# Scaling the first chunks from the weight's row in PSUM, and normalising retention outputs ahead of the state's split at first chunks

## The chip, the cores and the metric

The kernel runs on one core of one Trainium2 chip. The metric is the time of one execution on the device, in microseconds (us). The core has TensorE (PE) for matrix products and transpositions, VectorE (DVE), ScalarE (ACT) and GpSimd (POOL) for work by element, and SyncE (SP), which issues DMA transfers; ACT and POOL can issue them too. Each engine takes its instructions in its own order. PE writes into PSUM, which is divided into banks; DVE and ACT read it there. PE's products are made in a rounded fp32 type (`fp32r`): an operand is split into a high part and the remainder ("hi" and "lo"), and three products (hi·hi, lo·hi, hi·lo) are summed.

## The reference

Two layers, one of retention and one of sliding-window attention, over 1024 prompt rows and 8 decode rows of width 1024. The change is in the first stage and in the retention of layer 1:

```python
def rmsnorm(x, g):
    return x * lax.rsqrt(jnp.mean(x * x, axis=-1, keepdims=True) + EPS) * g

def retention_layer(x, S0, g_norm, w_in, g_out, w_out):
    h = rmsnorm(x, g_norm)                    # x 1024x1024 (prompt), 8x1024 (decode)
    q, k, v, gate = split(h @ w_in)           # widths 1024, 1024, 2048, 2048
    # 4 heads, chunks of 128 rows, per head and chunk:
    #   o_c = (q_c k_c^T * dmask) v_c + (q_c S) * cross_decay
    #   S   = S * chunk_decay + (k_c * k_decay)^T v_c
    o = rmsnorm(o, g_out)                     # per head, over 512 columns
    return x + (o * silu(gate)) @ w_out, S
```

The attention layer (16 query heads, 2 key heads, window 128, with sinks) follows; the change leaves its computation alone.

## The kernel before

**First stage.** The prompt is taken in 8 chunks of 128 rows (numbers 0 to 7); number 8 stands for the decode rows. A chunk is loaded (`xload`, L425, a DMA on SP's queue), squared and summed by ACT (`sq`, L430), its factor rsqrt(mean + eps) is made by POOL (`pw`, L434 and the power at L119), it is scaled by DVE with factor and gain (`sc`, L439), transposed by PE into two banks (`TR`, through the helper at L104), and split from there: `hi` by ACT (L456), `lo` by DVE (L460). The gain `norm_ret` comes as one row; PE multiplies it with a row of ones (L874), so that it stands in 128 partitions of the two banks `bank_of[0, 0]` and `bank_of[0, 1]`; DVE copies it from there to `gb` (L887). The decode rows are scaled like a chunk, and transposed by eight small transpositions into `p8`; `dcols` (L494, L495) appends columns of them to the operands of the products, and `rdec` keeps them all (L907). The first products of the projections are at L543; weights come into five slots of a pool (`raw_tile`, L176), and are split into `woh` (ACT, L220) and `wol` (POOL or DVE, L225).

The products of a group of output columns (a "set") are combined on DVE and ACT (`evac`, L363 to L379; the gate's SiLU at L382), and each output goes to scratch in DRAM (`spill`: for a gate set POOL applies the gain, L392, and copies the decode columns, L401; then SP issues the DMA `gsc<-raw`, L396). The last set's outputs lie in the `raw` slots, four of the five.

**Retention.** The heads go in two pairs, (0,1) and then (2,3), over 8 chunks each: 32 steps, in the order chunk by chunk with both heads of a pair. The work of a step is divided into small functions, and one loop (L1572) issues them for several steps at once, skewed:

| engine | functions (line) |
|---|---|
| PE | `b_qk` scores and transposition of k into the `tr` tile (L778, L104); `b_mm` state `S` (L1032 to L1034), output `po` (L1036 to L1045); `b_tr` transposition of the normalised output `on` |
| ACT | `b_kh` (L785), `b_sh` (L800), `b_vh` (L810), `b_qh` (L821), `b_Sh` split of the state (L1052), `b_sq` square of the output with sum (L1070), `b_oh` (L1105) |
| DVE | `b_kl` (L790), `b_sT` masked scores (L795), `b_Sl` (L1064), `b_ts` (L1074), `b_on` normalises (L1082), `b_og` times gate (L1098) |
| POOL | `b_sl` (L805), `b_vl` (L815), `b_ql` (L827), `b_pw` (power, L119), `b_ol` (L1110) |

In pass i of the loop PE's order is `b_qk(i+1)`, `b_mm(i)`, `b_tr(i-1)`; the other engines' order is set by `others(i)` (L1112): `b_og(i-2)`, the state and the norm of step i−1, the conversions of step i+1 (`CONV`) with `b_on(i-1)` after the first three, then `b_oh` and `b_ol` of step i−2. At a head's last chunk, and at a first chunk but the first of all, the norm's three functions stand ahead of the state's two. The order of ACT, DVE, POOL and SP is written out by hand: it is the order of issue in the code.

The first chunk of a head has no state to read, and the last one writes its state `sf` to the output by a DMA on ACT's queue (L1057). The `tr` tile has two slots (pool `trp`, L937), which the scores and transposition of k of one step and the transposed output of another take in turn. Steps 0 and 1 (`early`, L751) take their operands from tiles of the gate stage (`first`); from step 2 on, and for `on` and `ss` from the start, they lie in the pool `rp`, whose order in memory `lay` sets by hand (L1018):

```python
lay("Sh1", "Sl1", "sT0", "sTh0", "sTl0", "qh0", "ql0", "kh0", "kl0", "ss0", "ss1", "sT1", "on1", "kh1", "kl1",
    "pad", "on0", "vh0", "vl0", "sTh1", "sTl1", "qh1", "Sh0", "Sl0", "vh1", "vl1", "ql1")
```

A tile of `rp` waits for whatever lay on its words before, tile by tile (`reuse_waits="tile"`): at the beginning of retention those are tiles of the gate stage.

Of the kernel before, what the change touches and what calls it, by code (L numbers as in the profile page):

```python
# [7 lines left out]
F32 = mybir.dt.float32  # L8
F32R = mybir.dt.float32r
AF = mybir.ActivationFunctionType  # L10
ALU = mybir.AluOpType
PSUM = bass.MemoryType.PSUM
# [4 lines left out]
ND = 8  # L17
# [5 lines left out]
NCH = NP // C  # L23
# [44 lines left out]
def _trunk(ctx, tc, nc, a):  # L68
    x_prompt, x_sample, state_ret = a["x_prompt"], a["x_sample"], a["state_ret"]
    cache_k, cache_v = a["cache_k"], a["cache_v"]  # L70
    norm_ret, ret_out_norm, norm_swa = a["norm_ret"], a["ret_out_norm"], a["norm_swa"]
# [3 lines left out]
    y_p, y_s, nrp, nrs = a["y_p"], a["y_s"], a["nrp"], a["nrs"]  # L75
# [27 lines left out]
    def tr(out, in_, ident, start=True, stop=True):  # L103
        nc.tensor.matmul(out, in_, ident, is_transpose=True, start=start, stop=stop)  # L104


    ident = cp.tile([128, 128], F32, name="ident")
# [18 lines left out]
    B11, B21, T3, B22, T2, T1, T4 = range(7)  # L126
# [6 lines left out]
    dcp = sa.enter_context(tc.tile_pool(name="dcp", bufs=1, reuse_waits="tile"))  # L133
# [5 lines left out]
    vdp = sa.enter_context(tc.tile_pool(name="vdp", bufs=1, space=PSUM))  # L139
# [4 lines left out]
    rdec = rdec32[:, :, 0:ND]  # L144
# [13 lines left out]
    xq_ = ExitStack()  # L158
# [254 lines left out]
    junk = xq.tile([128, D], F32, name="junk")  # L413
    X, SS, PO = {}, {}, {}

    def xload(c):
        if c in (0, 1, 2):
            X[c] = xq.tile([128, D], F32, tag="xq", bufs=4, name="xq")
        elif c == 7:
            X[c] = raw_tile()  # L420
        elif c != 3:
            X[c] = sp.tile([128, D], F32, tag="u", bufs=3, name="u")
        if c == 8:
            X[c] = X[c][0:ND, :]
        nc.sync.dma_start(out=X[c], in_=x_sample[:, 0, :] if c == 8 else x_prompt[0, c * 128:c * 128 + 128, :])  # L425

    def sq(c):
        SS[c] = sp.tile([128, 1], F32, name="ss", bufs=4)
# [8 lines left out]
    def sc(c):  # L437
        n = X[c].shape[0]
        dve.scalar_tensor_tensor(X[c], X[c], SS[c][:n], gb[:n], MUL, MUL)  # L439

    def TR(c, b):

        PO[c] = [bank(b, j).rearrange("p (k t) -> p k t", k=4) for j in range(2)]
        for j in range(2):
            for k in range(4):
                tr(PO[c][j][:, k, :], X[c][:, 512 * j + k * 128:512 * j + k * 128 + 128], ident)
# [41 lines left out]
    def dcols(t, x, src=None):  # L488

        if src is None:  # L490
            k0, r0 = DB[x]
            src = rdec[:, k0:k0 + 4, r0 + 2 * t:r0 + 2 * t + 2]
        h = XH[t][x][:, :, 256:258]
        dve.tensor_copy(h, src)  # L494
        dve.tensor_tensor(XL[t][x][:, :, 256:258], src, h.bitcast(F32), SUB)  # L495
# [122 lines left out]
    n = 0  # L618
# [253 lines left out]
    for j in range(2):  # L872
        bank_of[0, j] = bank(0, j)
        mm(bank_of[0, j], row1, grow[:, 512 * j:512 * j + 512], start=True, stop=True)  # L874
    act(warm, warm, AF.Silu)
    for c in (0, 8, 2):
        xload(c)
    for r in range(2):
        raw_load(q0, r, nc.sync)
# [3 lines left out]
        raw_load(k0, r, nc.sync)  # L883
    for c in (4, 6, 7):
        xload(c)
    for j in range(2):
        dve.tensor_copy(gb[:, 512 * j:512 * j + 512], bank_of[0, j])  # L887
    for c in (0, 2, 8):
        sq(c)
        pw(c)  # L890
    sc(0)
    TR(0, 1)
    sc(2)
    TR(2, 2)
    sc(8)
    p8 = vdp.tile([128, 8, ND], F32, tag="vd", name="pd8")
    for k in range(8):
        tr(p8[:, k, :], X[8][:, k * 128:k * 128 + 128], ident[:ND, :ND])
    for j in range(2):
        hi(0, j)  # L900
        lo(0, j)
    w_hi(q0, "A11", 0)
    for j in range(2):
        hi(2, j)
    dcols(0, B11, p8[:, 0:4, 0:2])
    dcols(0, B21, p8[:, 4:8, 0:2])
    dve.tensor_copy(rdec, p8)  # L907
    for j in range(2):
        lo(2, j)
    w_lo(q0, "A11", 0, pool)  # L910
# [23 lines left out]
    print("stage", clock[0], "decode", t0)  # L934
    sa.close()
    tq = ExitStack()
    trp = tq.enter_context(tc.tile_pool(name="trp", bufs=2, space=PSUM))  # L937

    ap = ctx.enter_context(tc.tile_pool(name="ap", bufs=1, side="right", reuse_waits="tile"))
    SA = ap.tile([128, 8, 2 * NT], F32R, name="SA")  # L940
# [51 lines left out]
        else:  # L992
            pool.tensor_tensor(l_, src, h.bitcast(F32), SUB)

    spp = sb.enter_context(tc.tile_pool(name="spp", bufs=1, space=PSUM))
    ss_ = ExitStack()
    sSp = ss_.enter_context(tc.tile_pool(name="sSp", bufs=1, space=PSUM, side="right"))
    ogt = [rp0.tile([128, 4, 128], F32, name="og", tag="og%d" % n) for n in range(2)]
    rp = sb.enter_context(tc.tile_pool(name="rp", bufs=1, reuse_waits="tile"))
    rt[:] = [rp, trp]  # L1000
# [4 lines left out]
    def lay(*names):  # L1005
        for nm in names:
            if nm[:2] in ("Sh", "Sl"):
                state(nm[:2], int(nm[2]))
                continue
            if nm == "pad":  # L1010
                rp.tile([128, 72], F32, name=nm)
                continue
            n, k = nm[:-1], int(nm[-1])
            w = dict(on=DV, ss=1, sT=128, vh=DV, vl=DV, kh=DK, kl=DK, sTh=128, sTl=128, qh=256, ql=256)[n]
            t = rp.tile([128, w], F32 if n in ("on", "ss", "sT") else F32R, name=n, tag=nm)
            R.setdefault(n, [None, None])[k] = t.rearrange("p (f t) -> p f t", f=2) if n in ("qh", "ql") else t

    lay("Sh1", "Sl1", "sT0", "sTh0", "sTl0", "qh0", "ql0", "kh0", "kl0", "ss0", "ss1", "sT1", "on1", "kh1", "kl1",  # L1018
        "pad", "on0", "vh0", "vl0", "sTh1", "sTl1", "qh1", "Sh0", "Sl0", "vh1", "vl1", "ql1")
    mk["m"] += [M23[:, 0:128], M23[:, 128:256]]  # L1020
    epsg = M01[:, 288:292]

# [24 lines left out]
    def b_Sh(h, c):  # L1047
        d = heads[h]
        if c < NCH - 1:
            d["Sb"] = [state(nm, h % 2) for nm in ("Sh", "Sl")]  # L1050
            for f in range(2):
                act(d["Sb"][0][:, f], d["S"][f], AF.Copy, scale=GAM[h] ** (128.0 * (c + 1) - SREF))  # L1052
        else:
            sf = rp.tile([128, 2, DV], F32, tag="Sh%d" % (h % 2), name="sf")
            for f in range(2):
                act(sf[:, f], d["S"][f], AF.Copy, scale=GAM[h] ** SREF)
            nc.scalar.dma_start(out=nrp[0, 0, h].rearrange("(f p) e -> p f e", p=128), in_=sf)  # L1057

    def b_Sl(h, c):
        d = heads[h]  # L1060
# [51 lines left out]
    def others(i):  # L1112
        conv = [(fn, i + 1 if i + 1 > 1 else -1) for fn in CONV]
        state = [(b_Sh, i - 1), (b_Sl, i - 1)]
        norm = [(b_sq, i - 1), (b_ts, i - 1), (b_pw, i - 1)]
        turn = 0 <= i - 1 < NS and (steps[i - 1][1] == NCH - 1 or (steps[i - 1][1] == 0 and i > 2))
        for fn, n in ([(b_og, i - 2)] + (norm + state if turn else state + norm) + conv[0:3] +
                      [(b_on, i - 1)] + conv[3:] + [(b_oh, i - 2), (b_ol, i - 2)]):
            at_step(fn, n)

    def dec_gate():
# [28 lines left out]
    pq = {}  # L1150
# [375 lines left out]
    def p_open():  # L1526
        pp = ps_.enter_context(tc.tile_pool(name="pp", bufs=1, reuse_waits="tile"))

        def t512(name):
            return pp.tile([128, 4, 128], F32, name=name)  # L1530
        pq["rb"] = [pp.tile([128, 4, 256], F32, name="rb", tag=f"rb{j}") for j in range(2)]
        pq["dT"] = pp.tile([128, 7, 4, 4], F32, name="dT")
        pp.tile([128, 144], F32, name="pad")
        pq["xr"] = pp.tile([128, 16, 64], F32, name="xr")
        for key in "xp":
            pq["r" + key] = pp.tile([128, 516], F32, name="r" + key).rearrange("p (t n) -> p t n", t=2)
        s2b = t512("s2b")
        pq["s1b"] = t512("s1b")
        pq["s2ab"] = [t512("s2a"), s2b]
        w3 = pp.tile([128, 2, 4, 128], F32R, name="w3")  # L1540
        w = [pp.tile([128, 2, 4, 128], F32R, name=f"w{j}") for j in (0, 1, 2, 4)]
        pq["w"] = [[x[:, 0], x[:, 1]] for x in w[0:3] + [w3] + w[3:]]
        pq["s1a"] = t512("s1a")
        pq["b2"] = ps_.enter_context(tc.tile_pool(name="b2p", bufs=1, space=PSUM))
        pq["nw"] = 0
        pq["yz"] = [[v.rearrange("p k f -> p (k f)").rearrange("p (k n) -> p k n", k=2) for v in vs]
                    for vs in ((pq["s2ab"][0], pq["s1a"]), (pq["s2ab"][1], pq["s1b"]))]
# [74 lines left out]


    ctx.enter_context(tc.manual_schedule(engines={ET.Activation, ET.DVE, ET.Pool, ET.SP}))
    pjp = ctx.enter_context(tc.tile_pool(name="pjp", bufs=2, space=PSUM, side="right"))
    wp = ctx.enter_context(tc.tile_pool(name="wp", bufs=1, reuse_waits="tile"))

    pieces, flight, tick = [], [], [0]
# [124 lines left out]
    t16 = c2p.tile([16, 8], F32, name="t16")  # L1753
    e16 = c2p.tile([16, 8], F32, name="e16")

    scp = tq.enter_context(tc.tile_pool(name="scp", bufs=2, space=PSUM))
    msp = tq.enter_context(tc.tile_pool(name="msp", bufs=1, space=PSUM))
    kvp = ctx.enter_context(tc.tile_pool(name="kvp", bufs=1))
    atp = ctx.enter_context(tc.tile_pool(name="atp", bufs=1))
    atq = []  # L1760
# [687 lines left out]
        now()  # L2448
    tq.close()
    xq_ = ExitStack()  # L2450
    xyp = xq_.enter_context(tc.tile_pool(name="xyp", bufs=1, space=PSUM))
    pvp = xq_.enter_context(tc.tile_pool(name="pvp", bufs=1, space=PSUM))
    job()
    fill(ps, 1.0)
    xy = xy_tile()
# [99 lines left out]
        job(0)  # L2555
    xq_.close()
    tq = ctx.enter_context(ExitStack())
    trp = tq.enter_context(tc.tile_pool(name="trp", bufs=2, space=PSUM))
    msp = tq.enter_context(tc.tile_pool(name="msp", bufs=1, space=PSUM))
    attn[0] = False  # L2560
    drain(out)

# [37 lines left out]
```

## Time and profile before

| quantity | value |
|---|---|
| three runs | 1236.3, 1239.33 and 1242.99 us, median 1239.33 |
| profiled execution: time | 1237.02 us |
| profiled execution: span in the trace | 1235.2 us |
| PE busy | 1214.5 us (98%) |
| DVE, POOL, ACT busy | 741.2, 701.2, 588.8 us |
| first product of the projections starts | 14.42 us |
| PE idle before the transpositions of `on` of step 0, and of step 16 | 1.79 and 0.78 us |

The span is the stretch from the first to the last recorded instruction; the execution's own time is 1.8 us longer. "Idle before" an instruction is the time in which its engine had nothing to do just ahead of it, with what ended that time. A tile's name is the program's: `on` the normalised output, `S` the state, `po` the output in PSUM, `kh` and `kl` the two parts of k, `sT` the masked scores, `ss` sums and factors.

### The profile page before, as it was taken

The numbers are of one execution on the slowest core, as the hardware profiler recorded it, in microseconds if no ns is written. First come the engines' busy times: TensorE is split into PE (matmuls) and PEld (weight loads), VectorE is DVE, ScalarE is ACT, GpSimd is POOL, SyncE is SP. The second block draws the span as 40 slices with busy tenths as digits, with TensorE's granted clock in tenths as the row PEclk, the third lists the DMA queues.
The fourth block names the chain that finished last, engine by engine and source line by source line (L and its number), as shares of the span: only waits on it lengthen the run. The fifth ranks groups of instructions, "written<-read, shape, count | busy, mean of one in ns | idle before, by whom it ended". The sixth has DMA issues, their size and how long they took to land.

```text
span 1235.2 us, 29414 instructions
## 1 busy us (share of the span) xinstructions
PE 1214.5 (98%) x11297; PEld 1152.4 (93%) x11297; DVE 741.2 (60%) x1425; ACT 588.8 (48%) x1511; POOL 701.2 (57%) x763
## 2 busy tenths in 40 slices
PE   8999999999999999999999999999999999999898
PEld 7999999999999999988888999999989999999898
DVE  6954656556566667357676455677336676577432
ACT  6533444544545655368876123455554546544000
POOL 6654543545638889889877145682655548545010
PEclk9999999999999999999999999999999999999999
DMA  6313867768686775455687894685531447255364
GB/s 220 113 48 120 248 186 218 227 199 231 188 254 178 196 237 171 126 175 170 214 270 209 248 253 168 194 244 148 130 97 58 133 131 184 78 172 168 76 135 86
DMA packets 260027, 213.11 MB, mean 173 GB/s; under 512 B 72881, under 2 KB 230901, under 8 KB 259870
## 3 DMA queue, kind: packets, MB, share of 16 engines
q1 hardware_dynamic: 215376, 178.75, 49.2%
q10 hardware_dynamic: 44510, 32.47, 8.7%
q8 instruction: 89, 1.46, 0.5%
q14 instruction: 52, 0.43, 0.1%
HBM read 139.03 MB, written 73.17 MB: 172 GB/s over the span
## 4 chain that ended last, share of the span: by engine, by line
PE 88%; DMA 4%; DVE 3%; POOL 2%; issue 1%; ACT 1%; SPq 1%; ACTq 0%; POOLq 0%; DVEq 0%
PE S L1317 9%; PE b L334 8%; PE b L336 7%; PE b L335 7%; PE pj L1692 7%; PE pj L1694 6%; PE pj L1693 6%; PE b L327 4%; PE b L328 4%; PE b L329 4%; PE b L543 2%; PE xy L2052 2%; PE tr L104 2%; PE o L2110 2%; PE S L334 1%; PE S L335 1%
## 5 line engine op out<-in xcount | busy, mean ns | idle before, releaser
L334 PE MATMUL b<-xh,woh 128*128 128x258 f32 x784 | 223.4, 285 | 0.0
L336 PE MATMUL b<-xh,wol 128*128 128x258 f32 x784 | 222.2, 283 | 1.0 <-POOL wol L225 1.0
L335 PE MATMUL b<-xl,woh 128*128 128x258 f32 x784 | 221.9, 283 | 0.0
L1692 PE MATMUL pj<-SA,wh 128*128 128x384 f32 (+1 forms) x576 | 190.1, 330 | 3.5 <-DVE sq L2338 2.0
L1694 PE MATMUL pj<-SA,wl 128*128 128x384 f32 (+1 forms) x576 | 185.1, 321 | 0.0
L1693 PE MATMUL pj<-SA,wh 128*128 128x384 f32 (+1 forms) x576 | 184.4, 320 | 0.0
L334 PEld LDWEIGHTS b<-xh,woh 128*128 128x128 f32 x784 | 148.2, 189 | 4.1 <-issue 4.1
L336 PEld LDWEIGHTS b<-xh,wol 128*128 128x128 f32 x784 | 148.1, 189 | 1.4 <-POOL wol L225 1.4
L335 PEld LDWEIGHTS b<-xl,woh 128*128 128x128 f32 x784 | 148.8, 190 | 0.0
L225 POOL TENSOR_TENSOR wol<-raw,woh 128x512 fp32r<-128x512 f32 x51 | 66.6, 1313 | 119.5 <-ACT woh L220 108.3
L327 PE MATMUL b<-woh,xh 128*128 128x256 f32 x448 | 126.8, 283 | 0.0
L328 PE MATMUL b<-wol,xh 128*128 128x256 f32 x448 | 126.2, 282 | 0.0
L329 PE MATMUL b<-woh,xl 128*128 128x256 f32 x448 | 125.8, 281 | 0.0
L1692 PEld LDWEIGHTS pj<-SA,wh 128*128 128x128 f32 x576 | 108.6, 189 | 11.7 <-issue 5.8
L1693 PEld LDWEIGHTS pj<-SA,wh 128*128 128x128 f32 x576 | 109.0, 189 | 0.0
L1694 PEld LDWEIGHTS pj<-SA,wl 128*128 128x128 f32 x576 | 108.8, 189 | 0.0
L327 PEld LDWEIGHTS b<-woh,xh 128*128 128x128 f32 x448 | 84.4, 188 | 5.0 <-issue 2.9
L1650 POOL TENSOR_TENSOR wl<-wr,wh 128x512 fp32r<-128x512 f32 x48 | 63.0, 1322 | 38.2 <-DMA out_dram<-yo 17.3
L329 PEld LDWEIGHTS b<-woh,xl 128*128 128x128 f32 x448 | 84.4, 188 | 0.0
L328 PEld LDWEIGHTS b<-wol,xh 128*128 128x128 f32 x448 | 84.4, 188 | 0.0
L220 ACT ACTIVATE woh<-s 128x512 fp32r<-128x512 f32 x88 | 54.1, 624 | 60.3 <-POOL s L210 24.0
L225 DVE TENSOR_TENSOR wol<-s,woh 128x512 fp32r<-128x512 f32 x88 | 67.9, 775 | 21.3 <-ACT woh L220 21.0
(515 smaller groups left out, 3156.4 us busy)
## 6 DMA issues: line engine op xcount, KB each, us to landing
raw<-in_w_in_ret_dram ACTq DMA_DIRECT2D x44, 512.0 KB
st<-in_state_ret_dram SPq DMA_DIRECT2D x64, 256.0 KB
out_dram<-st SPq DMA_DIRECT2D x64, 256.0 KB
vb<-vscr SPq DMA_DIRECT2D x64, 128.0 KB
evp<-qks SPq DMA_DIRECT2D x32, 256.0 KB
evx<-vsc SPq DMA_DIRECT2D x32, 256.0 KB
wr<-in_w_in_swa_dram SPq DMA_DIRECT2D x32, 256.0 KB
pbs<-pb SPq DMA_DIRECT2D x16, 320.0 KB
```

The lines of the kernel that those rows point to most:

```text
L225: eng.tensor_tensor(lo, src_of(s, name, sub), hi.bitcast(F32), SUB)
L327: mm(dst, xh, wh, start=a and i == 0, stop=False, skip_group_check=True)
L328: mm(dst, xh, wl, start=False, stop=False, skip_group_check=True)
L329: mm(dst, xl, wh, start=False, stop=z, skip_group_check=True)
L334: mm(dst, wh, xh, start=a, stop=False, **sg)
L335: mm(dst, wh, xl, start=False, stop=False, **sg)
L336: mm(dst, wl, xh, start=False, stop=z, **sg)
L1317: mm(box[0], s.op[f"A{i + 1}{j + 1}", 0][w][:, k, :], xs_[t][x[j]][:, k, :], start=(xs_ is XH and w == 0 and j + k == 0), stop=(xs_ is XL ...
L1650: nc.gpsimd.tensor_tensor(box["lo"][:, js, :], raw, box["hi"].bitcast(F32)[:, js, :], ALU.subtract)
L1692: mm(ps, hi[:, k, fs], xh[:, k, t0:t1], start=first and k == ks[0], stop=False)
L1693: mm(ps, hi[:, k, fs], xl[:, k, t0:t1], start=False, stop=False)
L1694: mm(ps, lo[:, k, fs], xh[:, k, t0:t1], start=False, stop=last and k == ks[-1])
```

## The change

At the start:

- x8 (the decode rows) is loaded on ACT's queue instead of SP's, and with it, on the same queue, a new small tile `g8`: the gain as 8 rows of 128. The squares and factors come in the order 8, 0, 2 instead of 0, 2, 8.
- `g8` is transposed to `gk8` (128x8). The decode rows are scaled by their factor alone, transposed, and `rdec` is made from the transposed rows times `gk8`; `dcols` takes its columns from `rdec`.
- Chunks 0 and 2 are scaled in halves directly from the gain's row in PSUM (`sc_first`). The copies of the gain to `gb` go from DVE to ACT, one after each half of chunk 2.

In retention:

- In passes 1 and 17 (after the first chunk of head 0 and of head 2) the order is norm, `b_on`, then the state, then all conversions. The `b_oh` and `b_ol` of step 14 are issued in pass 17 instead of 16.
- `on0` lies first in `rp`.
- The final states `sf` are issued on SP's queue instead of ACT's.

Besides, the PSUM pools `trp`, `spp`, `sSp`, `b2p`, `pjp`, `scp`, `msp`, `xyp` and `pvp` (and `trp` and `msp` once more at the end) get `reuse_waits="tile"`.

```diff
-    def xload(c):
+    def xload(c, eng=nc.sync):
...
-        nc.sync.dma_start(out=X[c], in_=x_sample[:, 0, :] if c == 8 else ...)
+        eng.dma_start(out=X[c], in_=x_sample[:, 0, :] if c == 8 else ...)
...
+    def sc_first(c, j):
+        v = X[c][:, 512 * j:512 * j + 512]
+        dve.scalar_tensor_tensor(v, v, SS[c], bank_of[0, j], MUL, MUL)
...
+    xload(8, nc.scalar)
+    g8 = dcp.tile([8, 128], F32, name="g8")
+    nc.scalar.dma_start(out=g8, in_=norm_ret.rearrange("o (k p) -> (o k) p", p=128))
     act(warm, warm, AF.Silu)
-    for c in (0, 8, 2):
+    for c in (0, 2):
         xload(c)
...
-    for j in range(2):
-        dve.tensor_copy(gb[:, 512 * j:512 * j + 512], bank_of[0, j])
-    for c in (0, 2, 8):
+    for c in (8, 0, 2):
         sq(c)
         pw(c)
-    sc(0)
-    TR(0, 1)
-    sc(2)
-    TR(2, 2)
-    sc(8)
-    p8 = vdp.tile([128, 8, ND], F32, tag="vd", name="pd8")
+    p8 = vdp.tile([128, 9, ND], F32, tag="vd", name="pd8")
+    tr(p8[:, 8, :], g8, ident[:8, :8])
+    gk8 = dcp.tile([128, 8], F32, name="gk8")
+    dve.tensor_copy(gk8, p8[:, 8, :])
+    dve.tensor_scalar(X[8], X[8], SS[8][:ND], None, MUL)
     for k in range(8):
         tr(p8[:, k, :], X[8][:, k * 128:k * 128 + 128], ident[:ND, :ND])
+    for j in range(2):
+        sc_first(0, j)
+    TR(0, 1)
+    dve.tensor_tensor(rdec, p8[:, 0:8, :], gk8.unsqueeze(2).broadcast_to([128, 8, ND]), MUL)
+    for j in range(2):
+        sc_first(2, j)
+        act(gb[:, 512 * j:512 * j + 512], bank_of[0, j], AF.Copy)
+    TR(2, 2)
+    dcols(0, B11)
+    dcols(0, B21)
     for j in range(2):
         hi(0, j)
         lo(0, j)
     w_hi(q0, "A11", 0)
     for j in range(2):
         hi(2, j)
-    dcols(0, B11, p8[:, 0:4, 0:2])
-    dcols(0, B21, p8[:, 4:8, 0:2])
-    dve.tensor_copy(rdec, p8)
...
-    trp = tq.enter_context(tc.tile_pool(name="trp", bufs=2, space=PSUM))
+    trp = tq.enter_context(tc.tile_pool(name="trp", bufs=2, reuse_waits="tile", space=PSUM))
...
-    lay("Sh1", "Sl1", ..., "kl1", "pad", "on0", "vh0", ...)
+    lay("on0", "Sh1", "Sl1", ..., "kl1", "pad", "vh0", ...)
...
-            nc.scalar.dma_start(out=nrp[0, 0, h].rearrange("(f p) e -> p f e", p=128), in_=sf)
+            nc.sync.dma_start(out=nrp[0, 0, h].rearrange("(f p) e -> p f e", p=128), in_=sf)
...
-        turn = 0 <= i - 1 < NS and (steps[i - 1][1] == NCH - 1 or (steps[i - 1][1] == 0 and i > 2))
-        for fn, n in ([(b_og, i - 2)] + (norm + state if turn else state + norm) + conv[0:3] +
-                      [(b_on, i - 1)] + conv[3:] + [(b_oh, i - 2), (b_ol, i - 2)]):
+        on = [(b_on, i - 1)]
+        og = [(b_oh, i - 2), (b_ol, i - 2)]
+        if i in (1, NS // 2 + 1):
+            seq = norm + on + [(b_oh, i - 3), (b_ol, i - 3)] + state + conv + og
+        else:
+            turn = 0 <= i - 1 < NS and (steps[i - 1][1] == NCH - 1 or (steps[i - 1][1] == 0 and i > 2))
+            seq = (norm + state if turn else state + norm) + conv[0:3] + on + conv[3:] + (og if i != NS // 2 else [])
+        for fn, n in [(b_og, i - 2)] + seq:
             at_step(fn, n)
```

More of the change, by code (lines that the diff above doesn't have):

```diff
@@ L424, in xload @@
             X[c] = X[c][0:ND, :]
-        nc.sync.dma_start(out=X[c], in_=x_sample[:, 0, :] if c == 8 else x_prompt[0, c * 128:c * 128 + 128, :])
+        eng.dma_start(out=X[c], in_=x_sample[:, 0, :] if c == 8 else x_prompt[0, c * 128:c * 128 + 128, :])
     def sq(c):
@@ L993, in dec_cols @@
             pool.tensor_tensor(l_, src, h.bitcast(F32), SUB)
-    spp = sb.enter_context(tc.tile_pool(name="spp", bufs=1, space=PSUM))
+    spp = sb.enter_context(tc.tile_pool(name="spp", bufs=1, reuse_waits="tile", space=PSUM))
     ss_ = ExitStack()
-    sSp = ss_.enter_context(tc.tile_pool(name="sSp", bufs=1, space=PSUM, side="right"))
+    sSp = ss_.enter_context(tc.tile_pool(name="sSp", bufs=1, reuse_waits="tile", space=PSUM, side="right"))
     ogt = [rp0.tile([128, 4, 128], F32, name="og", tag="og%d" % n) for n in range(2)]
@@ L1016, in lay @@
             R.setdefault(n, [None, None])[k] = t.rearrange("p (f t) -> p f t", f=2) if n in ("qh", "ql") else t
-    lay("Sh1", "Sl1", "sT0", "sTh0", "sTl0", "qh0", "ql0", "kh0", "kl0", "ss0", "ss1", "sT1", "on1", "kh1", "kl1",
-        "pad", "on0", "vh0", "vl0", "sTh1", "sTl1", "qh1", "Sh0", "Sl0", "vh1", "vl1", "ql1")
+    lay("on0", "Sh1", "Sl1", "sT0", "sTh0", "sTl0", "qh0", "ql0", "kh0", "kl0", "ss0", "ss1", "sT1", "on1", "kh1", "kl1",
+        "pad", "vh0", "vl0", "sTh1", "sTl1", "qh1", "Sh0", "Sl0", "vh1", "vl1", "ql1")
     mk["m"] += [M23[:, 0:128], M23[:, 128:256]]
@@ L1543, in p_open @@
         pq["s1a"] = t512("s1a")
-        pq["b2"] = ps_.enter_context(tc.tile_pool(name="b2p", bufs=1, space=PSUM))
+        pq["b2"] = ps_.enter_context(tc.tile_pool(name="b2p", bufs=1, reuse_waits="tile", space=PSUM))
         pq["nw"] = 0
@@ L1624, in _trunk @@
     ctx.enter_context(tc.manual_schedule(engines={ET.Activation, ET.DVE, ET.Pool, ET.SP}))
-    pjp = ctx.enter_context(tc.tile_pool(name="pjp", bufs=2, space=PSUM, side="right"))
+    pjp = ctx.enter_context(tc.tile_pool(name="pjp", bufs=2, reuse_waits="tile", space=PSUM, side="right"))
     wp = ctx.enter_context(tc.tile_pool(name="wp", bufs=1, reuse_waits="tile"))
@@ L1754, in _trunk @@
     e16 = c2p.tile([16, 8], F32, name="e16")
-    scp = tq.enter_context(tc.tile_pool(name="scp", bufs=2, space=PSUM))
-    msp = tq.enter_context(tc.tile_pool(name="msp", bufs=1, space=PSUM))
+    scp = tq.enter_context(tc.tile_pool(name="scp", bufs=2, reuse_waits="tile", space=PSUM))
+    msp = tq.enter_context(tc.tile_pool(name="msp", bufs=1, reuse_waits="tile", space=PSUM))
     kvp = ctx.enter_context(tc.tile_pool(name="kvp", bufs=1))
@@ L2450, in _trunk @@
     xq_ = ExitStack()
-    xyp = xq_.enter_context(tc.tile_pool(name="xyp", bufs=1, space=PSUM))
-    pvp = xq_.enter_context(tc.tile_pool(name="pvp", bufs=1, space=PSUM))
+    xyp = xq_.enter_context(tc.tile_pool(name="xyp", bufs=1, reuse_waits="tile", space=PSUM))
+    pvp = xq_.enter_context(tc.tile_pool(name="pvp", bufs=1, reuse_waits="tile", space=PSUM))
     job()
@@ L2557, in _trunk @@
     tq = ctx.enter_context(ExitStack())
-    trp = tq.enter_context(tc.tile_pool(name="trp", bufs=2, space=PSUM))
-    msp = tq.enter_context(tc.tile_pool(name="msp", bufs=1, space=PSUM))
+    trp = tq.enter_context(tc.tile_pool(name="trp", bufs=2, reuse_waits="tile", space=PSUM))
+    msp = tq.enter_context(tc.tile_pool(name="msp", bufs=1, reuse_waits="tile", space=PSUM))
     attn[0] = False
```

## The prediction

> **What bounds the kernel now.** I read the page's head first, then busy time by stretch (PE's busy time with its count of matmuls, the granted clock, the DMA engines' share, GB/s), then TensorE's (PE's) timeline at the places that the diff touches.
>
> ```profile
> span 1235.2 us, 29414 instructions
> PE 1214.5 (98%) x11297; PEld 1152.4 (93%) x11297; DVE 741.2 (60%) x1425; ACT 588.8 (48%) x1511; POOL 701.2 (57%) x763
> ...
> 545.00:605.00 60.00, 60.00 (x328) 1.00 0.56 180
> ```
>
> PE is busy for 1214.5 of 1235.2 us, and the diff removes no matmul of it. So all that can be won or lost is PE's idle time: 20.7 us in the whole span, and only the part of it that lies at the start and at the two "first chunks" of the retention stage. Where PE is busy throughout (60.00 of 60.00 us between 545 and 605), a cheaper wait on another engine is worth nothing. PE's own gaps at the touched places are these:
>
> ```profile
> 3.31 3.75 PE L874 MATMUL b<-xq,row 1*128 1x512 f32 x4 [3.31 <-DMA xq<-in_norm_ret_dram]
> 14.42 2.06 PE L543 MATMUL b<-xh,woh 128*128 128x258 f32 x8 [0.35 <-DVE xh L494]
> ...
> 536.50 0.47 PE L1032 MATMUL S<-first 128*128 128x512 f32 x1 [0.61 <-DVE raw L379]
> 541.13 0.39 PE L1038 MATMUL po<-first 128*128 128x512 f32 x1
> 543.31 0.66 PE L104 MATMUL tr<-ident,on 128*128 128x128 f32 x4 [1.79 <-DVE on L1082]
> 543.80 0.63 PE L778 MATMUL tr<-evp 128*128 128x128 f32 x4
> ...
> 615.48 0.63 PE L104 MATMUL tr<-ident,on 128*128 128x128 f32 x4 [0.78 <-DVE on L1082]
> 615.94 0.61 PE L778 MATMUL tr<-evp 128*128 128x128 f32 x4
> ```
>
> The number in brackets is the idle time just before the instruction and what ended it. In retention that is 0.61 + 1.79 + 0.78 = 3.2 us, the most that the retention edits can win.
>
> **The start: squares, scaling, gain copies.** The edit takes two copies of the gain (L887) off DVE's way to the first scaling and puts two of them on ACT; it moves the load of the decode rows x8 from SP's queue to ACT's, and squares them first.
>
> ```profile
> 0.73 0.55 ACTq L867 DMA_DIRECT2D xq<-in_norm_ret_dram  x1
> 1.17 0.37 SPq L425 DMA_DIRECT2D u<-in_x_sample_dram  x1
> 5.00 1.06 ACT L430 ACTIVATE junk<-xq 128x1024 f32<-128x1024 f32 x1 [1.76 <-DMA xq<-in_x_prompt_dram]
> 6.51 0.56 POOL L119 TENSOR_TENSOR ss<-ss,mhalf 128x1 f32<-128x1 f32 x1
> 7.09 0.69 DVE L887 COPY gb<-b 128x512 f32<-128x512 f32 x1 [1.01 <-PE b L874]
> 8.01 1.28 DVE L439 SCALAR_TENSOR_TENSOR xq<-xq,ss,gb 128x1024 f32<-128x1024 f32 x1 [0.22 <-DVE gb L887]
> 9.74 1.28 DVE L439 SCALAR_TENSOR_TENSOR xq<-xq,ss,gb 128x1024 f32<-128x1024 f32 x1 [0.45 <-POOL ss L119]
> 12.37 1.32 ACT L456 ACTIVATE xh<-b 128x512 fp32r<-128x512 f32 x2
> 13.05 1.02 PE L104 MATMUL pd<-ident,u 8*128 8x8 f32 x8
> ...
> L785 ACT ACTIVATE kh<-tr,M x30: 455/475/477, 542.3 to 673.5; 128x256 fp32r<-128x256 f32 x30
>   DVE sT L795: 5.4, 26
> ```
>
> Work on chunk 0: its square began at 5.00 and its factor was there at 6.51 + 0.56 = 7.07, but DVE was copying the gain until 7.78. Without the copies it could scale at about 7.1: a gain of up to 0.9 us. Against it: the square of x8 (1.06 + 0.19 to read the sum) now stands ahead in ACT's order. x8 is issued on ACT's queue behind two other transfers, some 0.6 us later than at 1.17, and lands by about 4.4 at best (1.8 and the 2.58 from 0.73 to 3.31) and 5.4 at worst; so the square of chunk 0 begins at 5.6 to 6.6, its factor at 7.7 to 8.7. DVE has to scale x8 before (0.7, from 0.69 for a copy of half a chunk, to 1.27), after the row matmul's end at 7.06 and a small transposition and copy (0.4): done at 8.2 to 8.8. Chunk 0 is scaled (1.28 in two halves) by about 10.0 instead of 9.29, chunk 2 by 11.4 to 11.8 instead of 11.02.
>
> Then the new copies. They read the same bank of PSUM as the scaling of chunk 2. The line that I read for this is L785: the ACT read of a bank of PSUM waited 26 of 30 times for DVE's read of the same bank, though neither writes it. So I take it that ACT's two copies wait for DVE, one half each, and end at 12.0 to 12.4; queued behind them on ACT stand the conversions `hi` of chunk 0 (1.2), a weight's (0.62) and `hi` of chunk 2, of which the first ended at 13.0 before. After: 12.4 + 1.2 + 0.62 + 0.6 gives 14.8 at the late end and 14.4 at the early one, and the first product starts about there, 14.55 against 14.42. What is removed at the end (1.02 of small transpositions, and 0.35 behind them) was PE time that a waiting PE had to give anyway. If the copies do not wait, they run at about 10, `hi` starts as TR(0) ends, and the product can start at 13.0. Bounds: −1.5 to +0.8; I take **+0.1**, by L785. The first stage's later work on POOL and DVE moves with the first product.
>
> [...]
>
> **First chunk of the first heads (step 0's output, at 537 to 548).** Before, ACT split the state (`Sh`), then squared the output; DVE split twice (`Sl`), then normalised. Now norm and `on` come first, then the state, then the conversions of step 2.
>
> ```profile
> 538.69 1.08 ACT L1052 ACTIVATE Sh<-S 128x512 fp32r<-128x512 f32 x2 [1.88 <-PE po L1037]
> 540.88 0.60 ACT L1070 ACTIVATE on<-po 128x512 f32<-128x512 f32 x1 [1.11 <-PE S L1034]
> 542.85 1.08 ACT L1052 ACTIVATE Sh<-S 128x512 fp32r<-128x512 f32 x2
> 539.32 1.29 DVE L1064 SCALAR_TENSOR_TENSOR Sl<-S,Sh 128x512 fp32r<-128x512 f32 x2 [2.96 <-ACT Sh L1052]
> 541.60 0.21 DVE L1074 TENSOR_SCALAR ss<-ss,M 128x1 f32<-128x1 f32 x1 [0.99 <-ACT on L1070]
> 542.50 0.75 DVE L1082 TENSOR_SCALAR on<-po,ss 128x512 f32<-128x512 f32 x1 [0.49 <-POOL ss L119]
> 543.17 0.48 DVE L790 SCALAR_TENSOR_TENSOR kl<-tr,M,kh 128x256 fp32r<-128x256 f32 x1
> 540.17 0.18 POOL L401 COPY gdec<-raw 128x2 f32<-128x2 f32 x1
> 541.90 0.57 POOL L119 TENSOR_TENSOR ss<-ss,mhalf 128x1 f32<-128x1 f32 x1 [1.55 <-DVE ss L1074]
> 539.51 1.49 SPq L396 DMA_DIRECT2D gsc<-raw  x3
> ```
>
> In this run `Sl` was done before `on`, so the order alone did not hold `on`; what held it was the square, which waited until 540.88 for PE's S L1034: its target `on0` lay over operands of step 1. `on0` now lies at the head of the pool `rp`. By the sizes in the code that head lies over two of the five `raw` slots (they end up 136 words higher than before, through g8's 128 and gk8's 8). Those hold outputs of the last gate set until their spills have been read out. The spills' DMAs are the last row: three issues from 539.51. The second slot's is the first of them. Landing: not before 539.51 + 2.58 = 542.1 (the 2.58 is the shortest transfer here, the row's), and not after 542.85, since the second `Sh`, which lay on the same words, started then right behind its predecessor. I take 542.75 for the square, nearer the later end, since three spills and the loads behind them share DMA engines that are busy for 0.56 of the time in the stretch that follows. Then as before: +0.72 the sum's scaling, +1.62 to `on` (541.60 after 540.88; 542.50 after 540.88), so `on` runs 544.4 to 545.1. After it on DVE, by the new order: two `Sl` (1.29), `sT` (0.28), and `kl` after ACT's `kh` (0.46), 0.48: 547.6. PE then does the transpositions of `on` at 545.1 and waits with those of step 3's q and k, which need the slot that `kl` of step 2 frees, until 547.7. Before they began at 543.80: **+3.9**. Queued behind `kl` on DVE are only the gate product and step 1's `Sl`; SP and POOL wait for nothing new.
>
> Without the wait for the spills, the square runs at 538.8, but POOL's copies keep its power until 540.35, `on` is done at 541.7, then the same `Sl`, `sT`, `kh`, `kl` make 544.25 and PE goes on at 544.35: +0.5. At the low end, `on` done early enough and `kl` not on the way: −1.8 −0.6.
>
> [...] The rows here do not show the landing itself.
>
> **First chunk of the second heads (at 609 to 617).**
>
> ```profile
> 609.63 0.39 ACTq L1057 DMA_DIRECT2D out_dram<-sf  x1
> 611.73 0.68 PE L778 MATMUL tr<-evp 128*128 128x128 f32 x4 [0.26 <-PE tr L104]
> 613.18 1.29 DVE L1064 SCALAR_TENSOR_TENSOR Sl<-S,Sh 128x512 fp32r<-128x512 f32 x2 [0.53 <-ACT Sh L1052]
> 614.39 0.28 DVE L795 TENSOR_TENSOR sT<-tr,M 128x128 f32<-128x128 f32 x1
> 614.59 0.74 DVE L1082 TENSOR_SCALAR on<-po,ss 128x512 f32<-128x512 f32 x1
> ```
>
> Here the order does hold `on`: two `Sl` and `sT` stand ahead. Moved in front, `on` ends by about 613.8, before PE needs it at 614.7, and the 0.78 go; the 0.26 at 611.73 may too, as the issues of `sf` (0.4 to 0.5 each) leave ACT. But now `on` (0.74) and `Sl` push `sT` and so `kh` and `kl` to an end at 616.3, and step 19's transpositions start at 616.4 against 615.94: **+0.45**, bounds −1.0 (all of the waits go) to +1.0. The `sf` issues on SP add 0.4 us each ahead of that queue's loads, for which PE shows no wait there: 0; if such a load had no slack, 0.8. The skipped and repeated `og` conversions are moved by a step, with PE's reader far behind: 0.
>
> All other edits (pools that release by tile) stand where PE shows no gap: 0, bounds −0.5 to 0.
>
> **Sum.** +0.1 + 3.9 + 0.45 = +4.45. The profiled execution took 1237.02 us, so 1241.5 for such a one; the median of the three runs is 1239.33, so 1243.8 there. I give **1243.5**.
>
> **Rivals.**
> (A) The spills' wait does not bind: the raw slots are read out by then, or the tile lies elsewhere. The remaining terms are +0.1 + 0.5 + 0.45 = +1: 1240.3. For it: an order and a place are the only things that the code changes here, and a transfer's landing is not seen. Against: the second spill of that slot goes out only at 539.51. This is also the case in which the change gains nothing it aims at.
> (B) The edit works, faster: the 1.79, the 0.61, the 0.26 and the 0.78 go (3.4), and at the start the ACT copies run early (−1.5): 1234.4 to 1236. It decides if the square starts by 539 and `kl` of step 2 ends before PE has finished the transpositions of `on` (about 542.2). Against: `kl` follows `Sl` in the new order.
> [...]
>
> **How the numbers follow.** Forecast 0.42, (A) 0.25, (B) 0.17, (C) 0.16. The range: from 1235.5, inside (B), to 1248, (C) and its late bounds (start +0.8, second turn +1.0). 0.5% is 6.2 us, about what a measurement of this kernel can tell from no change: faster is below 1233.1, which only the far end of (B) reaches with the scatter of the runs (1236.3 to 1242.99), 0.10; slower is above 1245.5, most of (C) and the forecast's late bounds, 0.17; the same 0.73.
>
> **What would show it.** Forecast: at the first turn, ACT's square at L1070 (line moved) idle until a DMA of gsc, and PE's q transposition idle until DVE's kl, at about 547.7; at the second turn the same wait of about 1.2 us in place of the 0.78 before the transpositions of `on`; at the start, ACT's gain copies idle until DVE, and the first product at about 14.5. Wrong: if the square of step 0 starts at about 539 and no step waits on kl, (B); if the square does and kl still holds PE for half a us, (A); if matmuls after the gap take twice their 0.23, (C).

## The result and the profile after

The changed kernel takes 1246.26 us (median of 7 runs), the one before 1238.14 (7 runs): a ratio of 1.0066, with a 95% interval of 1.0051 to 1.0081. That is 8.1 us slower; 1243.5 was forecast. The profiled execution took 1246.35 us, against 1237.02. First the head of the page of the changed kernel, then PE's timeline at the places that the prediction showed (the line numbers of the shown rows are 4 to 16 higher than before).

```profile
span 1244.6 us, 29431 instructions
PE 1216.4 (98%) x11298; PEld 1152.9 (93%) x11298; DVE 741.3 (60%) x1426; ACT 589.3 (47%) x1513; POOL 699.5 (56%) x763
...
16.08 0.74 PE L547 MATMUL b<-xh,woh 128*128 128x258 f32 x4 [1.13 <-ACT xh L460]
52.34 1.07 PE L104 MATMUL b<-ident,raw 128*128 128x128 f32 x8 [0.31 <-DVE raw L439]
537.71 0.39 PE L1043 MATMUL S<-first 128*128 128x512 f32 x1
546.61 0.63 PE L104 MATMUL tr<-ident,on 128*128 128x128 f32 x4 [3.93 <-DVE on L1093]
548.98 1.19 PE L782 MATMUL tr<-evp 128*128 128x128 f32 x4 [1.75 <-issue]
623.89 0.68 PE L782 MATMUL tr<-evp 128*128 128x128 f32 x4 [1.65 <-issue]
712.32 1.23 PE L1333 MATMUL S<-SA,w 128*128 128x258 f32 x8 [0.44 <-ACT w L1201]
920.05 0.39 PE L1708 MATMUL pj<-SA,wh 128*128 128x264 f32 x1 [1.43 <-ACT qs L1929]
```

The wait of 0.61 us before the first S product is gone. At the first turn (step 0's output) 3.93 and 1.75 us stand in place of 1.79, and at the second (step 16's) 1.65 in place of 0.26 and 0.78. The start of the same work in both traces says where the time went:

| PE reaches | before | after | later by |
|---|---|---|---|
| the first product | 14.42 | 16.08 | 1.66 |
| the transpositions at 50 us | 50.07 | 52.34 | 2.27 |
| step 0's first S product | 536.50 | 537.71 | 1.21 |
| step 3's scores and transpositions | 543.80 | 548.98 | 5.18 |
| the same of step 5 | 553.00 | 560.56 | 7.56 |
| the same of step 20 | 620.55 | 628.56 | 8.01 |
| the first wait for `qs` in the next layer | 910.79 | 920.05 | 9.26 |
| the end of the span | 1235.2 | 1244.6 | 9.4 |

So in this pair of traces the start costs 2.3 us, and about 1.1 is won back before retention. The first turn costs 4.0, and 2.4 more come within the next two steps, where PE does not wait at all. The second turn costs 0.45, the rest of layer 1 1.25. The spans differ by 9.4 us, 1.3 more than the medians: the profiled execution of the kernel before was 1.1 us faster than its median.

Two rows of the table vary between traces of kernels that are alike up to there. At 50 us the six traces with the changed start lie at 52.13 to 52.40, the three with the start of before at 50.07 to 51.24: the start costs 0.9 to 2.3. And four of those six reach step 0's first S product at 536.29 to 536.59, over 1.1 us earlier than the one shown; in it PE waits 0.47 and 0.19 us near 462 and 483 for POOL's `wol`, in the four nowhere in that stretch.

**The start.** These are ACT's and DVE's timelines of the changed kernel.

```profile
1.74 0.34 ACTq L425 DMA_DIRECT2D u<-in_x_sample_dram  x1
7.00 1.06 ACT L430 ACTIVATE junk<-u 8x1024 f32<-8x1024 f32 x1 [3.02 <-DMA u<-in_x_sample_dram]
8.18 1.06 ACT L430 ACTIVATE junk<-xq 128x1024 f32<-128x1024 f32 x1
12.79 1.25 ACT L909 ACTIVATE gb<-b 128x512 f32<-128x512 f32 x2 [2.29 <-DVE xq L443]
13.94 1.08 ACT L460 ACTIVATE xh<-b 128x512 fp32r<-128x512 f32 x2
...
10.56 1.41 DVE L443 SCALAR_TENSOR_TENSOR xq<-xq,ss,b 128x512 f32<-128x512 f32 x2 [0.74 <-POOL ss L119]
```

x8, issued at 1.74, is there only at 7.00, and ACT sits idle for it for 3.02 us. So chunk 0's square starts at 8.18 instead of 5.00, and its scaling at 10.56 instead of 8.01. The copies of the gain wait for DVE (2.29) as foreseen, and `hi` follows them.

**The first turn.** ACT, DVE, SP in the changed kernel:

```profile
544.09 0.60 ACT L1081 ACTIVATE on<-po 128x512 f32<-128x512 f32 x1 [5.29 <-DMA gsc<-raw]
545.71 0.75 DVE L1093 TENSOR_SCALAR on<-po,ss 128x512 f32<-128x512 f32 x1 [0.69 <-POOL ss L119]
546.38 1.28 DVE L1075 SCALAR_TENSOR_TENSOR Sl<-S,Sh 128x512 fp32r<-128x512 f32 x2
548.40 0.48 DVE L794 SCALAR_TENSOR_TENSOR kl<-tr,M,kh 128x256 fp32r<-128x256 f32 x1 [0.54 <-ACT kh L789]
540.58 1.89 SPq L396 DMA_DIRECT2D gsc<-raw  x3
```

The square waits for a spill of the last gate set, by name: in the built program it waits for the four spills of the two `raw` slots under `on0`, and the last of these to be issued is the first of the three at 540.58. `kl` ends at 548.88, and step 3's transpositions start 0.1 us later: the "issue" in PE's bracket at 548.98 is this wait.

**PE's clock.** Busy time by stretch, PE's busy time, its matmuls and the granted clock (before, then after); below, two products of step 2 after the change.

```profile
545.00:565.00 20.00, 20.00 (x109) 1.00 0.61 196
```

```profile
545.00:565.00 20.00, 16.65 (x78) 0.83 0.48 151
...
550.83 0.63 PE L1044 MATMUL S<-vl,kh 128*128 128x512 f32 x1
551.25 0.63 PE L1045 MATMUL S<-vh,kl 128*128 128x512 f32 x1
```

Those two start 0.42 us apart, where they had 0.23 to 0.24 before the change. The granted clock is 0.83 in the mean of this stretch, against 1.00 before.

### The profile page after: what moved, and what is told of

It is laid out like the page before. It is cut to its first block, busy times and chain, and to the rows that moved or that the text cites. A ratio compares the mean times of both kernels' runs of the same rounds, so it can differ in the third digit from the quotient of the medians.

```text
span 1244.6 us, 29431 instructions
## 1 busy us (share of the span) xinstructions
PE 1216.4 (98%) x11298; PEld 1152.9 (93%) x11298; DVE 741.3 (60%) x1426; ACT 589.3 (47%) x1513; POOL 699.5 (56%) x763
## 4 chain that ended last, share of the span: by engine, by line
PE 86%; DMA 4%; POOL 3%; DVE 3%; issue 2%; ACT 1%; SPq 1%; ACTq 0%; POOLq 0%; DVEq 0%
PE S L1333 7%; PE b L334 7%; PE b L336 7%; PE b L335 7%; PE pj L1708 7%; PE pj L1710 6%; PE pj L1709 6%; PE b L327 4%; PE b L328 4%; PE b L329 4%; PE b L547 2%; PE tr L104 2%; PE xy L2068 2%; PE o L2126 2%; PE S L334 1%
```

## The experiments

Each kernel is the changed one with one edit, unless said otherwise. Times are medians, ratios are to the kernel before as run beside it, with 95% intervals. Differences of 1 to 2 us between medians are inside the scatter, so PE's timeline decides. Where a stretch is compared, it is from step 3's transpositions to step 19's, or up to the first wait for `qs` ("the next layer's wait", 920.05 in the changed kernel).

**on0 back in its old place.**

```diff
-    lay("on0", "Sh1", "Sl1", ..., "pad", "vh0", ...)
+    lay("Sh1", "Sl1", ..., "pad", "on0", "vh0", ...)
```

> The changed kernel with on0 back behind the pad in lay; all else stays. Theory (the head of rp lies on raw slots whose spills still run): the square of step 0 waits for step 1's last S product instead of the DMA gsc<-raw, so it starts at about 542.1 instead of 544.09; PE's gap before the transpositions of on falls from 3.93 to about 1.9 us, the wait of 1.75 us behind them (for kl, by the order) stays, and PE's clock stays full in 545:560 (it was 0.77), which is worth 2.4 us: 4.4 us less than the changed kernel in all, about 1242. Rival (the new order alone is the cause, the place does not matter): gap and time as in the changed kernel, about 1246.

1244.41 us, ratio 1.0055 (1.0034 to 1.0077). PE's rows and the clock:

```profile
543.29 0.65 PE L104 MATMUL tr<-ident,on 128*128 128x128 f32 x4 [1.87 <-DVE on L1093]
545.82 1.19 PE L782 MATMUL tr<-evp 128*128 128x128 f32 x4 [1.87 <-issue]
...
545.00:565.00 20.00, 19.18 (x90) 0.83 0.47 154
```

The gap falls from 3.93 to 1.87 us, so the place is what made the square wait so long, and the second gap stays. But the clock fell all the same, to 0.83 over 545 to 565, against the expectation: here two gaps of 1.87 with 0.65 us of work between them were enough. The time is 2.4 us above the expected 1242, as much as the full clock had been put at.

**on0 where nothing late lies.**

```diff
+    lay("Sh1", "kh1", "sTh1", "on0", "Sl1", ...)
```

> The changed kernel with on0 laid behind Sh1, kh1 and sTh1, over the raw slot that holds no output of the last set. Theory: the square starts as step 0's output is done (about 540), then POOL's gain copies hold the power until about 542.3, on ends at 543.7, PE's gap is about 1.1 us; then Sl, sT, kh and kl in the new order still make PE wait, until about 546.3 instead of 548.98: 2.7 us, and 2.4 us of the clock, so about 1241, still above before. Rival 1 (the wait for spills was all that was wrong): no wait for kl either, about 1238 or less. Rival 2 (the place does not matter): 1246.

1240.88 us, 1.0026 (1.0009 to 1.0043).

```profile
542.55 0.63 PE L104 MATMUL tr<-ident,on 128*128 128x128 f32 x4 [1.12 <-DVE on L1093]
544.92 1.20 PE L782 MATMUL tr<-evp 128*128 128x128 f32 x4 [1.75 <-issue]
```

The gaps are the expected 1.1 and 1.75: without any wait for spills the new order still costs the wait for `kl`, and the kernel stays slower than before. The last wait of `on` is POOL's power, behind the gain copies. The clock fell here too (transpositions of 1.20 instead of 0.61, a mean of 0.86 over 545 to 565), which I had not expected. The median came out at the forecast 1241 nevertheless; the trace is of a slower execution (1243.67), and what made up for the clock is not shown.

**The old order, on0 still in front.**

```diff
-        if i in (1, NS // 2 + 1):
-            seq = norm + on + [(b_oh, i - 3), (b_ol, i - 3)] + state + conv + og
...
+        turn = 0 <= i - 1 < NS and (...)       # others() as before
```

> The changed kernel with the old order in passes 1 and 17 (others() of before); on0 stays at the head of rp. Theory: the gap before the transpositions of on stays near 3.9 us since the square still waits for gsc<-raw, but step 3's transpositions follow at once (1.75 us less), the clock may still fall, and the second turn has its 0.78 us instead of 1.65 (0.5 less net): about 1244. Rival (the order is the whole cause): the gap falls back to 1.8 us and the time to about 1240.

1242.16 us, 1.0042 (1.0028 to 1.0057).

```profile
545.23 1.09 PE L104 MATMUL tr<-ident,on 128*128 128x128 f32 x4 [3.67 <-DVE on L1093]
618.85 0.63 PE L104 MATMUL tr<-ident,on 128*128 128x128 f32 x4 [0.37 <-DVE on L1093]
```

The gap of 3.67 remains without the order, and the second gap is gone with it: place and order are two separate costs at the first turn. At the second turn only 0.37 is left, where the kernel before has 0.26 and 0.78. What differs most there from the kernel before is the queue of `sf`; the last two kernels below come back to it. The time is 1.8 us below the expected 1244; in this trace step 0's first S product comes at 536.59, 1.1 earlier than in the changed kernel's.

**PE kept busy in the gap.**

```diff
         on = d.pop(("on", c))
+        if (h, c) == (0, 0):
+            for i in range(30):
+                tr(pt[:, 0:128], ident, ident)
```

> The changed kernel with 30 more transpositions of 0.115 us (3.45 us) into the tile of step 0's transposed output ahead of the four real ones, which overwrite it: they fill PE's idle gap and wait for nothing. Theory (the idle gap lowers PE's clock): granted clock 1.00 in 545:560, the products of step 2 take 0.23 us from start to start instead of 0.43, the waits stay where they are, 2.4 us less: about 1244. Rival (the products are slow from another cause, or the clock falls in the second gap of 1.75 alone): no change, 1246.

1245.34 us, 1.0059 (1.0036 to 1.0082).

```profile
541.10 3.44 PE L104 MATMUL tr<-ident 128*128 128x128 f32 x30
546.07 0.66 PE L104 MATMUL tr<-ident,on 128*128 128x128 f32 x4 [1.53 <-DVE on L1093]
548.54 0.68 PE L782 MATMUL tr<-evp 128*128 128x128 f32 x4 [1.81 <-issue]
...
545.00:565.00 20.00, 17.12 (x94) 1.00 0.49 166
```

The waits end where they did, the clock stays full, and from step 3's transpositions to step 19's it takes 72.59 us instead of 74.91: the idle time of 3.93 us lowered the clock (0.83 over 545 to 565, against 1.00 with the filler), and that cost 2.3 us. The median moved by 0.9 only, less than it can resolve; the trace lost 1.1 us again by the next layer's wait and more behind it.

**The start of before.**

```diff
-    xload(8, nc.scalar)
-    g8 = dcp.tile([8, 128], F32, name="g8")
...
+    for c in (0, 8, 2):       # and all of the start as before
```

> The changed kernel with the start of before (squares 0, 8, 2, all loads on SP, gain copied by DVE first). Theory (the new start costs 2.0 us that nothing behind gives back): the first product at 14.4 instead of 16.1, step 0's scores 2.0 us earlier, the rest as in the changed kernel: 2.0 us less, about 1244.3. Rival (the start's loss is absorbed by later waits): 1246.

1245.16 us, 1.0058 (1.0036 to 1.0079). The first product starts at 13.89, 2.2 us earlier, step 0's first S product 1.5 and step 3's transpositions only 0.9 earlier. So 0.7 of the start's loss vanished before retention, and 0.6 at the turn, where the square started at 543.15 against 544.09, still behind the transfers; the truth lies between theory and rival. Here, and in the kernel with `sf` on ACT below, the row of the square names the load of `M`, issued right behind the spills, where the six other traces with `on0` in front name `gsc<-raw`; in the built program of the changed kernel, and of the one with `sf` on ACT, the square waits for the spills and not for `M`.

**x8 first on SP's queue.**

```diff
-    xload(8, nc.scalar)
+    xload(8)
```

> The changed kernel with x8 loaded first on SP's queue instead of third on ACT's. Theory (x8's landing at 7.00 holds all three squares): the squares begin at about 4 to 5 us, chunk 0 is scaled some 1.5 us earlier (then held by g8's landing at 7.5 and by x0), and the first product starts at about 14.6 instead of 16.08: 1.4 us less, about 1245. Rival (the price lies in squaring x8 first, or in ACT's copies of the gain): the first product moves by less than 0.5.

1244.26 us, 1.0049 (1.0034 to 1.0064).

```profile
3.51 1.04 ACT L430 ACTIVATE junk<-u 8x1024 f32<-8x1024 f32 x1
13.54 0.75 PE L547 MATMUL b<-xh,woh 128*128 128x258 f32 x4 [1.00 <-ACT xh L460]
```

x8 is there by 3.51, with no wait, and the first product comes 2.54 us earlier than in the changed kernel and 0.9 earlier than before: this one landing accounts for the whole loss of the start. It lasts, too: step 0's first S product comes at 533.68, 2.6 us or more earlier than in any trace with the changed start. Squaring x8 first did no harm here, with x8 there by 3.51.

**x8 first on ACT's queue.**

```diff
+    xload(8, nc.scalar)
     nc.scalar.dma_start(out=grow, in_=norm_ret[0:1, :])
```

> The changed kernel with x8 first on ACT's queue, ahead of the gain's row and the identity. Theory (x8 lands late because transfers of 512 KB that were issued before it fill the DMA engines, not because of the queue it is on): x8 lands by 3.5 to 4, the squares follow from there, and the first product starts at 13.5 to 14.0 instead of 16.08. Rival (ACT's queue is slow beside SP's): x8 lands at 6 or later, the first product at 15.5 or later.

1243.83 us, 1.0059 (1.0038 to 1.008).

```profile
3.88 1.05 ACT L430 ACTIVATE junk<-u 8x1024 f32<-8x1024 f32 x1
5.13 3.75 PE L879 MATMUL b<-xq,row 1*128 1x512 f32 x4 [5.13 <-DMA xq<-in_norm_ret_dram]
15.24 2.23 PE L547 MATMUL b<-xh,woh 128*128 128x258 f32 x8 [0.75 <-ACT xh L460]
```

It is the order of issue and not the queue: on ACT's queue x8 lands by 3.88 too. But now the gain's row, issued 0.7 us later than before, lands at 5.13 instead of 2.3, and the first product at 15.24 fits neither number. In these traces a small transfer issued 0.7 to 1.4 us after the first load of 512 KB is usable only 3.7 us (the gain's row), 5.3 (x8) or 5.4 us (g8 in the changed kernel) after its own issue.

**The gain's copies later.**

```diff
-        act(gb[:, 512 * j:512 * j + 512], bank_of[0, j], AF.Copy)    # behind sc_first(2, j)
...
     for j in range(2):
         hi(2, j)
+    for j in range(2):
+        act(gb[:, 512 * j:512 * j + 512], bank_of[0, j], AF.Copy)
```

> The changed kernel with ACT's two copies of the gain moved behind the hi conversions of chunk 2. Theory (the copies wait for DVE's scaling of chunk 2 and hold up hi): hi of chunk 0 starts at about 12.8 instead of 13.94, the first product at about 14.9 instead of 16.08: 1.2 us less, about 1245. Rival (hi would wait for the transpositions of chunk 0 anyway): less than 0.4.

1246.2 us, 1.0076 (1.0051 to 1.0101).

```profile
12.51 0.60 ACT L460 ACTIVATE xh<-b 128x512 fp32r<-128x512 f32 x1 [2.02 <-PE b L104]
16.20 0.75 PE L547 MATMUL b<-xh,woh 128*128 128x258 f32 x4 [1.18 <-ACT gb L919]
```

`hi` starts 1.4 us earlier, and the first product not at all: now PE waits for the copies themselves. The row names them as the releaser; in the built program the first product writes the bank of PSUM that held the gain's row. The rival's number came out (less than 0.4), but not by its reason; both missed this wait. The copies' end is on the first product's way in both places tried.

**sf on ACT's queue again.**

```diff
-            nc.sync.dma_start(out=nrp[0, 0, h]..., in_=sf)
+            nc.scalar.dma_start(out=nrp[0, 0, h]..., in_=sf)
```

> The changed kernel with the sf transfers back on ACT's queue. Theory (on SP they delay the loads of the output projection's weights): the gaps of 0.44 and 0.22 us at 712 go, and the 1.2 us between retention's end and the first product of the next stage: about 1245. Rival (that difference is a knock-on of the 8 us shift, or differs from run to run): 1246, the same gaps.

1247.66 us, 1.0082 (1.0063 to 1.0101). The gaps at 712 are gone, and from step 19's transpositions to the next layer's wait it takes 295.60 us, against 296.16 in the changed kernel and 294.85 before. So this explains half of the 1.25 us at most. Over all fourteen traces of this document the stretch takes 294.85 to 295.82 in the four with `sf` on ACT and 295.96 to 298.43 in the ten with `sf` on SP, which speaks for the queue. Against the theory's mechanism, the gaps at 712 do not follow it: they are absent with the filler (`sf` on SP), and two of 0.15 and 0.23 stand there in the kernel "start mended" below (`sf` on ACT). The time did not fall. What the other half is stays open.

**The pools alone** (the kernel before with `reuse_waits="tile"`, nothing else).

> The kernel before with nothing of the change but reuse_waits=tile on the PSUM pools. Theory: the 0.61 us before step 0's first S product goes, and nothing is late next, as the square still waits for step 1's S and the transpositions of on for it: within 1 us of before, 1237 to 1238. Rival (the pools' waits release more than this gap): 1235 or less; rival (the released work collides elsewhere): slower than before.

1238.27 us, 0.9999 (0.9984 to 1.0013): no change. The 0.61 is gone; the gap before step 0's transposed output is 1.85 instead of 1.79. The start, which this kernel shares with the one before, was at 15.63 in this trace and at 14.42 in the other: the same start moved by 1.2 us between these two executions.

**Start mended, rest as before** (x8 on SP, copies late, old order, old place, `sf` on ACT), and **the same with on0 in the free place and sf on SP**.

> The changed kernel with x8 first on SP's queue, the gain's copies behind hi of chunk 2, and the order, the place of on0 and the queue of sf as before. Theory: first product at 13.5 to 14 instead of 14.42 in before, retention as in before with the pools' 0.6 us: 1 to 1.5 us less than before, about 1237. Rival (g8's landing or the order of the squares still holds the start): 1238 to 1239, no better than before.

> The order of before, x8 first on SP, the gain's copies behind hi of chunk 2, tile-wise pools, sf on SP, and on0 behind Sh1, kh1 and sTh1, where the square waits for no spill and no product of step 1. Theory: PE's gap before step 0's transposed output falls from 1.85 to about 1.1 us (POOL's copies still hold the power) with no wait for kl behind it, the second turn's gaps from 0.93 to 0.4 (as in the run with the old order, where sf was on SP), first product at 13.6 instead of 14.42: about 1.3 us less in the trace than the kernel with on0 and sf as before, some 3 us less than the kernel before up to the next stage; in the time 1235 to 1237. Rival (sf on SP delays the next stage's weights by as much as it wins): 1238.

1238.63 us, 1.0009 (0.9996 to 1.0021), and 1236.65 us, 0.9993 (0.9979 to 1.0008). The second one's two turns:

```profile
539.78 0.63 PE L104 MATMUL tr<-ident,on 128*128 128x128 f32 x4 [1.13 <-DVE on L1094]
611.49 0.63 PE L104 MATMUL tr<-ident,on 128*128 128x128 f32 x4 [0.35 <-DVE on L1094]
```

Both gaps came out as expected (the first of the two kernels, with `sf` on ACT, still had 0.26 and 0.67 at the second turn), no wait for `kl` follows, and the first product starts at 13.56. The next layer's wait ends at 908.73 and 908.25, against 910.79 before: 2.1 and 2.5 us won in the traces. In the time neither is shown to be faster. From that wait to the end of the span the traces of all kernels take between 324.1 and 327.3 us (324.4 before, 326.4 in the first of these two, 324.4 in the second), with no order that I can see; that scatter hides 2 us.

What the move of `sf` is worth at the second turn depends on the order. From step 17's transpositions to step 19's, PE takes 6.95 us in both kernels with the old order and `sf` on SP, and 7.58 to 7.83 in the three with the old order and `sf` on ACT. No two of these differ in the queue alone (the last two kernels differ in the place of `on0` too), so this win of 0.6 to 0.9 us is likely but not isolated. With the new order it is 8.21 with `sf` on SP and 8.23 on ACT: in the change as it was made, the move won nothing there.

## Why the prediction was right, and where it was not

The direction, the range and the mechanism of the largest term held; four terms did not: the start, the clock, the pools and the stretch behind retention. The time is 2.8 us above the forecast, and "slower", above 1245.5, had been given only 0.17.

- **First turn.** Right in mechanism and size. The spill that the forecast named, the first of the three, was issued at 540.58, and the square started at 544.09; from the square's start to step 3's transpositions it took 4.89 us, where the forecast had 4.95 (542.75 to 547.7). The turn cost 4.0 us against the kernel before, forecast 3.9. From that issue to the square's start the rows have 3.5 us, and 3.2 to 4.1 in seven traces with `on0` in front, where the forecast had 3.2 (539.51 to 542.75).
- **Second turn.** +0.45 forecast; +0.45 measured (7.56 to 8.01). The wait of about 1.2 us came as 1.65, with the 0.26 ahead of it gone; with `sf` on ACT it is 1.19 with 0.25 ahead of it, to the same end.
- **The start.** The term +0.1 (bounds −1.5 to +0.8) was mis-sized: 1.66 us at the first product, twice its late bound. The failed step is "lands by about 4.4 at best and 5.4 at worst". I took x8's landing from the gain row's 2.58 us, a transfer that nothing had been issued ahead of; x8 went out behind two chunks of 512 KB and took 5.3 us. Put first, on SP, it was there 2.8 us after its issue at the latest (0.73 to 3.51), and PE's first product came 2.54 us earlier. The copies on ACT did wait for DVE (2.29 us), as read from the L785 rows.
- **The clock.** Case (C), matmuls after the gap at twice their 0.23, given 0.16 as a case of its own, came true on top of the forecast: step 2's products start 0.42 us apart instead of 0.23, at a granted clock of 0.83 in the mean of 545 to 565. The range's upper end of 1248 takes some 1246 for (C). What that counts for the clock is shown by no run; the filler showed 2.3 us (72.59 against 74.91). That 1246 is the measured time, but partly by luck: the start's 1.7 and the 1.25 behind retention are not in it, nor the 1.1 won before retention, nor that the median before came down from 1239.33 to 1238.14 with seven runs. By what the filler shows, the clock belonged in the sum as a term with a chance, since the forecast itself had PE wait until 545.1 and again until 547.7.
- **The pools.** "Stand where PE shows no gap: 0" is wrong: PE showed the 0.61 ahead of step 0's first S product, and the pools alone removed it. The time did not move by it.
- **Behind retention.** 1.25 us were lost up to the next layer, where `sf` on SP had been put at 0 for want of a wait in the trace of before, and at 0.8 if a load had no slack. The queue accounts for half of it at most.
- **Rival (A)** was met by the kernel with on0 in the free place: the wait for `kl`, put at +0.5 net, was 1.75 with a gap of 1.1 ahead, net 1.2 (8.46 us from step 0's first S product to step 3's transpositions, against 7.30). The kernel ended 3.4 us above before, with the late start and the fallen clock in it.
- **Rival (B)** would have needed `kl` early; every run with the new order shows it late.

In the traces 9.4 us were lost where 4.45 were forecast: 2.2 more at the start, 2.4 by the clock, 1.25 behind retention and 0.2 elsewhere, less the 1.1 won before retention.

## What to carry to other kernels

When an engine's work is moved ahead, look at what it passes: here DVE's normalisation went ahead, and the state's split, moved behind it, held the next step's k, for which PE waited 1.75 us. A tile's place in memory is an order of its own: moving a tile off one late reader can put it on a later one (the square of step 0 went from 540.88 to 544.09), and the address arithmetic shows it before a run does. And in these traces a small load that starts a chain belongs ahead of the big ones in the order of issue, on either of the two queues tried (x8 there by 3.51 and 3.88 instead of 7.00), as long as it does not push another such load behind them, as x8 did with the gain's row on ACT's queue (5.13 instead of 2.33).

## What the runs showed of the hardware

- PE's granted clock fell after idle time that was interrupted: after 1.12 and 1.75 us with 0.63 us of transpositions between them its mean was 0.86 over 545 to 565, while after a single gap of 1.79 to 1.85 it was full (1.00 in three kernels). With 3.44 us of filler ahead, it was full after 1.53 and 1.81 too (1.00). Gaps of 3.81 and 3.93 left the next four transpositions at full speed (0.63), and those of 3.67 and 4.07 to 4.50 did not (1.08 to 1.09): a gap's length alone did not decide it, and what did is not shown. How much work between gaps keeps the clock up was not tried.
- A 32 KB load issued 1.0 us after the first 512 KB load took 5.3 us to be usable; issued ahead of it on the same queue, 2.8 at most. The gain's row took 1.5 to 2.6 us when issued along with that load and 3.7 when issued 0.7 us later.
